# A streaming encoder step on one core: the scan's factors prepared in two parts beside the products, its widest level in two strips, and one gate block earlier in the order

## The chip, the core and the metric

The kernel runs on one core of one Trainium2 chip. The metric is device time in microseconds (us), the median of the runs shown. One program computes the whole step in one launch.

## The reference, cut to what matters

The step is one encoder layer for a prompt of 1024 rows and a sample of 64 rows, 1024 features wide. The combined projection `h @ w_in` feeds three groups of heads; the change is in the first, the gated scan of four heads with 128 features each:

```
def step(s, inp):                                  # one chunk of the sequence, one head
    qc, kc, vc, gc = inp
    G = cumsum(gc)                                 # running sum of log decay
    o = (qc * exp(G)) @ s                          # what the state gives
    att[t, u] = sum_k qc[t,k] * exp(G[t,k] - G[u,k]) * kc[u,k]    for u <= t
    o = o + att @ vc
    s_new = exp(G[-1]) * s + (kc * exp(G[-1] - G)).T @ vc
```

Afterwards each row of `o` is normalised and multiplied with a gate `silu(ag)`. The second group of heads has a gate `bg`, the third a gate `cg`, both also blocks of the combined projection.

## The kernel before, in words

**Order of the work.** Tasks are Python generators. A planner (`Sched`) keeps a planned clock for each engine, adds a written cost for every instruction, and always continues the first task whose inputs are ready on those clocks. The main task issues the projections: for each block of 128 weight columns (`names`, line 676) three chunks of columns (384, 384 and 320) with 24 matmuls each, three products (high and low halves) per 128 features. These are the rows `mm<-hhi,whi`, `mm<-hlo,whi` and `mm<-hhi,wlo`. They go out in batches of six, and between batches a scan task may put its own work. After that a tile scheduler fixes the place of each instruction on its engine.

**The scan of one head** (`hgrn`, line 364) is spawned when `ai` of its head has been projected and starts when V of the head stands in rows (`v{h}`). It has three groups: group 0 and 1 are four chunks of 128 prompt rows, group 2 is the sample's 64 rows. For each group:

- `prep` makes the factors. `G` is the running sum (line 383), `M = lnk - G`. For each level b of 64, 32, 16, 8, 4 and 2 a tile `E` gets its first halves from M and its second halves from G (two adds on DVE), goes through Exp on ACT, and its second halves are multiplied with q on DVE. Then come `k`, `qf` (with a copy of q on POOL, line 404), `Kh`, `eL` and `Qh` (which takes the place of G).
- `pe1` multiplies on PE. "pB" means one chunk's block of 32x32 products: 16 products `hg<-E` of the levels 16 to 2 and four `hg<-qf,k`; each counts twice in the trace (32 and 8). "pA" means the products of the levels 64 and 32 for all chunks: per chunk one 64x64 product and two 32x32 products. Four pB come first, with a planned pause of 0.9 us behind each, then pA, then four transposes of `Kh`. DVE turns pB into `AT` by a mask (`msk`), a sum (line 449) and a spread; ACT copies pA into `AT` and the transposed `Kh` into `Kt`.
- `pe2a` makes the states S by `V,Kt` and a chain on DVE; `pe2b` makes the output by `V,AT` and `S,G` and starts its norm: four squares on ACT (`o_sb`), two steps on POOL (`small`, lines 318 and 321), a product on DVE (`o_sb`); `pe3` transposes `o_sb` and applies the gate.

pA, pB, the states and the output all take banks of one PSUM tag, `hg`, with three buffers. `E` has seven buffers, `G` two, `M`, `k`, `qf` and `Kh` one.

**What a head's work follows.** The order is prep(0), pe1(0), prep(1), pe2a(0), pe2b(0), pe1(1), prep(2), pe2a(1), pe3(0), pe2b(1), pe1(2), pe3(1), pe2a(2), pe2b(2), pe3(2). The main task stops at `af` of head j until the scan of head j-2 has ended, and at `cg` j until that of head 1+j has ended. The gate blocks `cg` 0 and 1 and `bg` 0 and 1 stand behind the four heads' blocks.

Of the kernel before, what the change touches and what calls it, by code (L numbers as in the profile page):

```python
# [104 lines left out]
def hybrid_step(  # L105
# [47 lines left out]
    def ps_hg():  # L153
        return ps.tile([P, 512], F32, tag="hg", name="hg", bufs=3)
# [22 lines left out]
    def act(out, in_, func, **kw):  # L177
        t = TABLE.get(func)
        sw = 1.3 if t is not None and t != cur.get("table") else 0.0
        if t is not None:  # L180
            cur["table"] = t
        sch.op("ACT", 0.2 + sw + free(in_) / 1200.0)
        cur['ACT'] = ACT.activation(out, in_, func, **kw)  # L183

    def tt(out, a, b, op):
        sch.op("DVE", 0.07 + free(out) / 960.0)
        cur['DVE'] = DVE.tensor_tensor(out=out, in0=a, in1=b, op=op)  # L187

    def stt(out, a, s, b, op0, op1):
        sch.op("DVE", 0.07 + free(out) / 960.0)  # L190
        DVE.scalar_tensor_tensor(out=out, in0=a, scalar=s, in1=b, op0=op0, op1=op1)
# [9 lines left out]
    def sub(out, a, b):  # L201
        tt(out, a, b, ALU.subtract)
# [110 lines left out]
    def rstd_of(ms, n, w=1, more=None):  # L313

        r = small()
        sch.op("POOL", 0.6)
# [4 lines left out]
        POOL.tensor_tensor(out=r[:n, :w], in0=r[:n, :w], in1=mhalf[:n, :w], op=ALU.pow)  # L321
        return r
# [39 lines left out]


    def hgrn(h, st, hp, hgc):
        yield f"v{h}"
# [3 lines left out]
        S0 = hp([P, P], F32, "S0", 1)  # L369
        SP.dma_start(S0, state_hgrn[0, 0, h])  # L370
        ctxs = {}

        def prep(gi):
            t0, width, csz, v0 = groups[gi]
            nch = width // csz
            lf, lk, qq = logf[:, t0:t0 + width], lnk[:, t0:t0 + width], q[:, t0:t0 + width]

            def g(tag, bufs=1):
                return hp([P, 512], F32, tag, bufs)[:, :width]

            G = g("G", 2)
            sch.op("DVE", 0.07 + width / 480.0)
            DVE.tensor_tensor_scan(G, reset[:, :width], lf, 0.0, ALU.mult, ALU.add)
            M = g("M")
            sub(M, lk, G)
            Gc = G.rearrange("p (c t) -> p c t", t=csz)
            E = {}
            for b in LEVELS:
                if 2 * b > csz:
                    continue  # L390
                nb = width // (2 * b)
                e = g("E", 7)
                ev, gv, mv, qv = [x.rearrange("p (n two b) -> p n two b", two=2, b=b) for x in (e, G, M, qq)]
                ref = gv[:, :, 0, b - 1:b].broadcast_to([P, nb, b])
                tt(ev[:, :, 0, :], mv[:, :, 0, :], ref, ALU.add)
                tt(ev[:, :, 1, :], gv[:, :, 1, :], ref, ALU.subtract)
                act(e, e, AF.Exp)
                stt(ev[:, :, 1, :], ev[:, :, 1, :], QSCALE, qv[:, :, 1, :], ALU.mult, ALU.mult)
                E[b] = e
            k = g("k")  # L400
            act(k, lk, AF.Exp)
            qf = hp([P, 2, 512], F32, "qf")[:, :, :width]
            sch.op("POOL", 0.1 + width / 1000.0)
            POOL.tensor_copy(qf[:, 1, :], qq)  # L404
            act(qf[:, 0, :], lf, AF.Exp)
            stt(qf[:, 0, :], qf[:, 0, :], QSCALE, qq, ALU.mult, ALU.mult)
            Kh = g("Kh")
            tt(Kh.rearrange("p (c t) -> p c t", t=csz), M.rearrange("p (c t) -> p c t", t=csz),
               Gc[:, :, csz - 1:csz].broadcast_to([P, nch, csz]), ALU.add)
            act(Kh, Kh, AF.Exp)  # L410
            eL = hp([P, 4], F32, "eL", 2)
            act(eL[:, :nch], Gc[:, :, csz - 1], AF.Exp)
            Qh = G
            act(Qh, G, AF.Exp)
            stt(Qh, Qh, QSCALE, qq, ALU.mult, ALU.mult)
            ctxs[gi] = dict(E=E, k=k, qf=qf, Kh=Kh, eL=eL, Qh=Qh, qq=qq)

        def pause(us):

            sch.cur.dep["EV"] = sch.t["PE"] + us  # L420
            yield None

        def pe1(gi):

            t0, width, csz, v0 = groups[gi]
            nch, nq = width // csz, csz // 32
            x = ctxs[gi]
            E, k, qf, qq = x["E"], x["k"], x["qf"], x["qq"]
            AT = hp([P, 4, P], F32, "AT", 1)
            for c0 in range(0, nch, 2):  # L430
                cn = min(2, nch - c0)
# [17 lines left out]
                DVE.tensor_reduce(out=dg[:csz, :cn], in_=msk[:csz, :cn].rearrange("p c l t -> p c t l"), axis=AX.X,  # L449
                                  op=ALU.add)  # L450
# [3 lines left out]
            pA = ps_hg().rearrange("p (c t) -> p c t", t=P)  # L454
            for c in range(nch):
                o = c * csz
                if csz == P:
                    mm(pA[0:64, c, 64:128], E[64][:, o:o + 64], E[64][:, o + 64:o + 128], True, True)
                for s in range(0, csz, 64):
                    mm(pA[s:s + 32, c, s + 32:s + 64], E[32][:, o + s:o + s + 32], E[32][:, o + s + 32:o + s + 64],  # L460
                       True, True)
# [62 lines left out]
        prep(0)  # L524
        yield None
        yield from pe1(0)
        prep(1)
        yield None
        pe2a(0, None)
        yield None  # L530
        pe2b(0)
        yield from pe1(1)
        prep(2)
        yield None
        pe2a(1, ctxs[0]["S"][-1])
# [134 lines left out]
    def main():  # L670
# [724 lines left out]
```

## Time and profile before

| What | Value |
|---|---|
| median of 3 runs (lowest, highest) | 945.51 us (944.09, 945.72) |
| the profiled execution | 946.23 us |
| its span, first to last instruction | 944.5 us |
| mean granted TensorE clock | 0.996 of full speed |
| PE busy over the span | 98% |
| the scan's products on PE | about 158 to 436 us |

The profiled execution's time is 1.7 us more than its span. PE busy is an overlap of pipelined matmuls: in a stream of 384 columns a matmul is shown as 0.34 us long while the next one begins 0.17 us later. What a piece of work costs PE is therefore read from the starts of the rows around it, not from its busy time. PEclk is the share of full clock that PE was granted. "Idle before" in brackets behind a row says how long the engine had nothing in flight, and who released it.

### The profile page before, as it was taken

How to read it: one execution, taken by the hardware profiler on the slowest of the kernel's cores; microseconds unless marked ns; L12 is line 12 of the kernel's file. 1: busy time of each engine (PE TensorE's matmuls, PEld its weight loads, DVE VectorE, ACT ScalarE, POOL GpSimd, SP SyncE). 2: the span in 40 equal slices, each digit the busy share in tenths (PEclk: the TensorE clock that was granted, in tenths of full speed). 3: DMA queues.
4: the chain of work that ended last, by engine and by line, in shares of the span. 5: the costliest groups of instructions: out<-in, count | busy, mean ns of one | idle time of the engine just before them, and what ended most of it. 6: DMA issues, size and time to landing. Idle time of an engine off the chain costs nothing.

```text
span 944.5 us, 18234 instructions
## 1 busy us (share of the span) xinstructions
PE 923.9 (98%) x7440; PEld 863.0 (91%) x7440; DVE 554.9 (59%) x1125; ACT 474.7 (50%) x1002; POOL 106.7 (11%) x194
## 2 busy tenths in 40 slices
PE   8999999999999999999999999999999999999997
PEld 6899999999988998998879778999999999999997
DVE  7849472548648636663485678555574455573343
ACT  7623382957435746992574766343453333342231
POOL 5503330001001001000000000212110000001110
PEclk9999999999989999999999999999999999999999
DMA  8806410101010111011110420222542011232221
GB/s 306 270 20 198 144 45 25 46 24 54 24 46 9 46 38 41 24 46 62 57 37 32 145 74 25 89 90 90 168 123 88 25 45 46 68 112 90 90 94 64
DMA packets 33126, 73.60 MB, mean 78 GB/s; under 512 B 5601, under 2 KB 18065, under 8 KB 33042
## 3 DMA queue, kind: packets, MB, share of 16 engines
q1 hardware_dynamic: 30112, 68.07, 22.5%
q0 software_dynamic: 1888, 4.35, 1.3%
q8 instruction: 58, 0.95, 0.4%
q14 instruction: 26, 0.21, 0.1%
q10 hardware_dynamic: 1042, 0.01, 0.1%
HBM read 56.45 MB, written 15.89 MB: 77 GB/s over the span
## 4 chain that ended last, share of the span: by engine, by line
PE 83%; DVE 6%; DMA 4%; ACT 2%; issue 2%; POOL 2%; DVEq 0%; POOLq 0%; ACTq 0%
PE mm L171 64%; PE hg L171 15%; PE tp L175 5%; DVE sm L587 3%; DVE sm L187 1%; DVE wlo L187 1%; POOL small L321 1%; DMA wraw<-in_w_xk_dram 1%; DMA xt<-in_x_prompt_dram 1%; DMA mkd<-mraw 1%; DMA gT<-in_norm_mem_dram 1%; DMA wraw<-in_w_xv_dram 1%; DMA mvd<-mtm 0%; ACT whi L183 0%; DVE hlo L187 0%
## 5 line engine op out<-in xcount | busy, mean ns | idle before, releaser
L171 PE MATMUL mm<-hhi,whi 128*128 128x384 f32 (+2 forms) x1272 | 421.8, 332 | 0.0
L171 PE MATMUL mm<-hlo,whi 128*128 128x384 f32 (+2 forms) x1272 | 413.2, 325 | 0.0
L171 PE MATMUL mm<-hhi,wlo 128*128 128x384 f32 (+2 forms) x1248 | 406.0, 325 | 0.0
L171 PEld LDWEIGHTS mm<-hhi,whi 128*128 128x128 f32 x1272 | 239.5, 188 | 4.5 <-issue 1.1
L171 PEld LDWEIGHTS mm<-hlo,whi 128*128 128x128 f32 x1272 | 239.6, 188 | 1.2 <-issue 1.1
L171 PEld LDWEIGHTS mm<-hhi,wlo 128*128 128x128 f32 x1248 | 234.7, 188 | 0.5 <-issue 0.3
L183 ACT ACTIVATE whi<-wraw 128x1024 fp32r<-128x1024 f32 (+1 forms) x53 | 55.1, 1041 | 82.5 <-PE mm L171 66.9
L187 DVE TENSOR_TENSOR wlo<-wraw,whi 128x1024 fp32r<-128x1024 f32 (+1 forms) x53 | 63.6, 1202 | 44.3 <-ACT whi L183 44.0
L183 ACT ACT_TABLE_LOAD x63 | 80.8, 1283 | 6.1 <-issue 2.0
L183 ACT ACTIVATE wraw<-mm 128x384 f32<-128x384 f32 (+3 forms) x51 | 22.9, 450 | 72.7 <-PE mm L171 62.7
L587 DVE TENSOR_TENSOR_SCAN sm<-sm 128x384 f32<-128x384 f32 (+4 forms) x52 | 48.2, 936 | 14.3 <-ACT sm L183 14.3
L183 ACT ACTIVATE sm<-hg 128x384 f32<-128x384 f32 (+4 forms) x104 | 42.3, 485 | 16.2 <-PE hg L171 9.1
L187 DVE TENSOR_TENSOR wraw<-mm,gain 128x384 f32<-128x384 f32 (+1 forms) x48 | 24.4, 509 | 41.7 <-ACT wraw L183 41.5
L1176 POOL TENSOR_TENSOR small<-small 128x1 f32<-128x1 f32 (+1 forms) x18 | 4.2, 234 | 373.9 <-ACT wraw L183 373.9
L171 PE MATMUL mm<-mhi,wlo 128*128 128x256 f32 x128 | 36.0, 289 | 2.6 <-DVE wlo L187 2.5
L171 PEld LDWEIGHTS hg<-E 128*32 128x32 f32 (+1 forms) x1288 | 24.9, 113 | 14.2 <-issue 6.4
L321 POOL TENSOR_TENSOR small<-small,mhalf 128x1 f32<-128x1 f32 (+2 forms) x50 | 36.6, 733 | 4.2
L171 PE MATMUL mm<-mhi,whi 128*128 128x256 f32 x128 | 36.1, 289 | 0.6 <-ACT mhi L183 0.6
L171 PE MATMUL hg<-E 128*32 128x32 f32 (+1 forms) x1288 | 33.7, 203 | 1.7 <-DVE o_sb L187 1.7
L171 PE MATMUL mm<-mlo,whi 128*128 128x256 f32 x128 | 35.0, 282 | 0.0
L404 POOL COPY qf<-q 128x512 f32<-128x512 f32 (+1 forms) x12 | 14.1, 1179 | 181.9 <-PE hg L171 168.2
L187 DVE TENSOR_TENSOR wlo<-C,whi 128x1024 fp32r<-128x1024 f32 x16 | 19.6, 1225 | 25.1 <-ACT whi L183 23.6
(209 smaller groups left out, 1426.3 us busy)
## 6 DMA issues: line engine op xcount, KB each, us to landing
wraw<-in_w_in_dram SPq DMA_DIRECT2D x28, 512.0 KB, 3.6
xt<-in_x_prompt_dram SPq DMA_DIRECT2D x8, 512.0 KB, 6.5
wraw<-in_w_xv_dram SPq DMA_DIRECT2D x8, 512.0 KB, 4.1
wraw<-in_w_out_dram SPq DMA_DIRECT2D x8, 512.0 KB, 3.6
C<-in_x_prompt_dram SPq DMA_DIRECT2D x8, 512.0 KB, 3.6
x1d<-C SPq DMA_DIRECT2D x8, 512.0 KB, 2.9
wraw<-in_w_xq_dram SPq DMA_DIRECT2D x8, 512.0 KB, 3.6
wraw<-in_w_xo_dram SPq DMA_DIRECT2D x8, 512.0 KB, 3.5
```

What stands on the lines that cost most here:

```text
L171: cur['PE'] = PE.matmul(out, lhsT=lhsT, rhs=rhs, start=start, stop=stop, skip_group_check=True)
L175: PE.transpose(out, in_, ident[:n, :n])
L183: cur['ACT'] = ACT.activation(out, in_, func, **kw)
L187: cur['DVE'] = DVE.tensor_tensor(out=out, in0=a, in1=b, op=op)
L321: POOL.tensor_tensor(out=r[:n, :w], in0=r[:n, :w], in1=mhalf[:n, :w], op=ALU.pow)
L404: POOL.tensor_copy(qf[:, 1, :], qq)
L587: DVE.tensor_tensor_scan(m[:nq, :n][:, ::-1], m[:nq, :n][:, ::-1], m[:nq, :n][:, ::-1], 1.0 if p is None else p[:nq, 0:1], ALU.mult, ALU.min)
L1176: POOL.tensor_tensor(out=ms[:n, 0:1], in0=ms[:n, 0:1], in1=ms[:n, pi:pi + 1], op=ALU.add)
```

## The change

1. `prep` is cut in two. `prepA` makes G, M and the three widest levels, `prepB` the three narrow levels, `Kh`, `k`, `qf`, `eL` and `Qh`. Within a part all adds are issued first, then the Exp, then the products. `beside` gives a part its own planned readiness, so that the head's products don't wait for it in the plan.
2. `pe1` is cut in two. `pe1a` (pA) comes first and needs only the two widest levels; a pause; then `pe1b` (the four pB, the transposes).
3. The 64x64 product of pA becomes two products with 32 of its columns each (two strips of 32 output partitions).
4. The order is now pe1a(0), prepA(1), pe1b(0), pe2a(0), pe2b(0), prepB(1), pe1a(1), prepA(2), pe1b(1), pe2a(1), pe3(0), pe2b(1), prepB(2), pe1a(2), pe1b(2), and so on. prepA(0) of the next head may begin once pe1a(2) of this head is out, prepB(0) once pe2a(2) is; both before `v{h}`.
5. `bg` 0 moves from behind `cg` to behind head 1's blocks. Its three chunks of 24 matmuls follow `ag` 1.
6. The planned cost of the norm's POOL step grows with the number of columns; the copy of q on POOL loses its planned cost.

The products and their operands are the same apart from point 3; the number of ACT table loads goes from 63 to 66. From the first transposes of `kr` behind the scan on, PE's order is the same row for row.

```diff
+        def levels(gi, bs):
...
+            for b in bs:
+                e = buf(gi, "E", 7)
...
+                tt(ev[:, :, 0, :], mv[:, :, 0, :], ref, ALU.add)
+                tt(ev[:, :, 1, :], gv[:, :, 1, :], ref, ALU.subtract)
+                vs.append((e, ev, qv, sch.t["DVE"]))
...
+            for e, ev, qv, at in vs:
+                sch.fresh(DVE=at)
+                act(e, e, AF.Exp)
...
+                stt(ev[:, :, 1, :], ev[:, :, 1, :], QSCALE, qv[:, :, 1, :], ALU.mult, ALU.mult)
+        def prepA(gi):
...
+            DVE.tensor_tensor_scan(G, reset[:, :width], lf, 0.0, ALU.mult, ALU.add)
+            M = buf(gi, "M")
+            sub(M, lk, G)
...
+            levels(gi, split_levels(gi)[0])
+        def pe1a(gi):
...
+                    for i in range(0, 64, 32):
+                        mm(pA[i:i + 32, c, 64:128], E[64][:, o + i:o + i + 32], E[64][:, o + 64:o + 128], True, True,
+                           0.045)
...
-                    mm(pA[0:64, c, 64:128], E[64][:, o:o + 64], E[64][:, o + 64:o + 128], True, True)
...
+        if h:
+            yield ("wide", h - 1)
+        beside(prepA, 0)
+        if h:
+            yield ("narrow", h - 1)
+        beside(prepB, 0)
+        yield f"v{h}"
...
+        pe1a(0)
+        beside(prepA, 1)
+        yield from pause(0.9)
+        yield from pe1b(0)
...
         names += [("af", h), ("aq", h), ("ai", h), ("ag", h)]
-        names += [("cg", 0), ("cg", 1), ("bg", 0), ("bg", 1)]
+            if h == 1:
+                names += [("bg", 0)]
+        names += [("cg", 0), ("cg", 1), ("bg", 1)]
```

**PE, head 1, group 1, before:** the last two of four pB (`hg<-E 32x32 x16` with `hg<-qf,k`) and the start of pA (`hg<-E 64x64`).

```order
L171 MATMUL hg<-E 32x32 x16
L171 MATMUL hg<-qf,k 32x64 x4
L171 MATMUL hg<-E 32x32 x16
L171 MATMUL hg<-qf,k 32x64 x4
L171 MATMUL hg<-E 64x64
L171 MATMUL hg<-E 32x32 x2
L171 MATMUL hg<-E 64x64
```

The same place now: pA (`hg<-E 32x64 x2` are the two strips) between projection matmuls.

```order
L171 MATMUL mm<-hhi_107,wlo 128x384
L171 MATMUL hg<-E 32x64 x2
L171 MATMUL hg<-E 32x32 x2
L171 MATMUL hg<-E 32x64 x2
L171 MATMUL hg<-E 32x32 x2
L171 MATMUL hg<-E 32x64 x2
L171 MATMUL hg<-E 32x32 x2
L171 MATMUL hg<-E 32x64 x2
L171 MATMUL hg<-E 32x32 x2
L171 MATMUL mm<-hhi_109,whi 128x320
```

Before, the four pB and pA stood in one run right behind the output products of group 0; now pA stands alone, each pB has at least six projection matmuls on either side, and the transposes stand apart.

**DVE, head 2, group 0, before:** what stands ahead of the first `msk` of the group (`M<-fl,G` and `E<-M,G` belong to group 1; `wlo`, `L` and `fl` to the main task).

```order
L187 TENSOR_TENSOR M<-fl,G 128x512
L191 SCALAR_TENSOR_TENSOR G<-G,q 128x512
L187 TENSOR_TENSOR E<-M,G 128x4x64
L187 TENSOR_TENSOR wlo<-wraw,whi 128x1024
L199 COPY fl<-mm 128x320
L187 TENSOR_TENSOR E<-G 128x4x64
L191 SCALAR_TENSOR_TENSOR L<-fl,L 128x1088
L191 SCALAR_TENSOR_TENSOR E<-E,q 128x4x64
L187 TENSOR_TENSOR fl<-L,fl 128x1088
L187 TENSOR_TENSOR msk<-hg,fmask 128x384
```

The same place now (L416 is the running sum):

```order
L416 SCALAR_TENSOR_TENSOR G<-reset,L 128x512
L187 TENSOR_TENSOR M<-fl,G 128x512
L187 TENSOR_TENSOR E<-G 128x4x64
L187 TENSOR_TENSOR E<-M,G 128x4x64
L187 TENSOR_TENSOR E<-M,G 128x8x32
L187 TENSOR_TENSOR E<-G 128x8x32
L187 TENSOR_TENSOR E<-M,G 128x16x16
L187 TENSOR_TENSOR E<-G 128x16x16
L191 SCALAR_TENSOR_TENSOR E<-E,q 128x4x64
L191 SCALAR_TENSOR_TENSOR E<-E,q 128x8x32
L187 TENSOR_TENSOR msk<-hg,fmask 128x384
```

Six adds of group 1 and two of its products now stand ahead of group 0's `msk`, in the place of one level of group 1 and work of the main task.

**POOL, head 1, before:** the copies of q for group 2 and for the next head's group 0, ahead of the norm of group 1 (`small 128x4`).

```order
L404 COPY qf<-q 128x64
L404 COPY qf<-q 128x512
L318 TENSOR_SCALAR small<-small 128x4
L321 TENSOR_TENSOR small<-small,mhalf 128x4
L318 TENSOR_SCALAR small<-small 64x1
```

The same place now:

```order
L443 COPY qf<-q 128x64
L318 TENSOR_SCALAR small<-small 128x4
L321 TENSOR_TENSOR small<-small,mhalf 128x4
L443 COPY qf<-q 128x512
L318 TENSOR_SCALAR small<-small 64x1
```

The long copy for the next group went behind the norm of group 1 and stands ahead of that of group 2.

More of the change, by code (lines that the diff above doesn't have):

```diff
@@ L315, in rstd_of @@
         r = small()
-        sch.op("POOL", 0.6)
+        sch.op("POOL", 0.3 + 0.25 * w)
         if more is None:
@@ L364, in hgrn @@
     def hgrn(h, st, hp, hgc):
-        yield f"v{h}"
         logf, lnk, q, V = st["logf"], st["lnk"], st["q"], st["V"]
@@ L368, in hgrn, with beside, factors_of @@
         groups = [(0, 512, P, 0), (512, 512, P, 4), (SEQ, SMP, SMP, 8)]
-        S0 = hp([P, P], F32, "S0", 1)
-        SP.dma_start(S0, state_hgrn[0, 0, h])
         ctxs = {}
-        def prep(gi):
+        def beside(f, gi):
+            save = sch.cur.dep
+            sch.fresh(**ctxs.setdefault(gi, dict(dep={}))["dep"])
+            f(gi)
+            ctxs[gi]["dep"], sch.cur.dep = sch.cur.dep, save
+        def factors_of(gi):
+            for e, v in ctxs[gi]["dep"].items():
+                sch.cur.dep[e] = max(v, sch.cur.dep.get(e, 0.0))
@@ new lines, in buf @@
+        def buf(gi, tag, bufs=1):
+            return hp([P, 512], F32, tag, bufs)[:, :groups[gi][1]]
+        def levels(gi, bs):
+            x = ctxs[gi]
+            width = groups[gi][1]
+            vs = []
+            for b in bs:
+                e = buf(gi, "E", 7)
+                ev, gv, mv, qv = [y.rearrange("p (n two b) -> p n two b", two=2, b=b)
+                                  for y in (e, x["G"], x["M"], x["qq"])]
+                ref = gv[:, :, 0, b - 1:b].broadcast_to([P, width // (2 * b), b])
+                tt(ev[:, :, 0, :], mv[:, :, 0, :], ref, ALU.add)
+                tt(ev[:, :, 1, :], gv[:, :, 1, :], ref, ALU.subtract)
+                vs.append((e, ev, qv, sch.t["DVE"]))
+                x["E"][b] = e
+            ends = []
+            for e, ev, qv, at in vs:
+                sch.fresh(DVE=at)
+                act(e, e, AF.Exp)
+                ends.append(sch.t["ACT"])
+            for (e, ev, qv, _), at in zip(vs, ends):
+                sch.fresh(ACT=at)
+                stt(ev[:, :, 1, :], ev[:, :, 1, :], QSCALE, qv[:, :, 1, :], ALU.mult, ALU.mult)
@@ new lines, in split_levels @@
+        def split_levels(gi):
+            bs = [b for b in LEVELS if 2 * b <= groups[gi][2]]
+            return bs[:3], bs[3:]
+        def prepA(gi):
+            t0, width, csz, v0 = groups[gi]
+            lf, lk, qq = logf[:, t0:t0 + width], lnk[:, t0:t0 + width], q[:, t0:t0 + width]
+            G = buf(gi, "G", 2)
+            sch.op("DVE", 0.07 + width / 480.0)
+            DVE.tensor_tensor_scan(G, reset[:, :width], lf, 0.0, ALU.mult, ALU.add)
+            M = buf(gi, "M")
+            sub(M, lk, G)
+            ctxs[gi].update(G=G, M=M, qq=qq, lf=lf, lk=lk, E={})
+            levels(gi, split_levels(gi)[0])
@@ L374, in prep, with prepB @@
+        def prepB(gi):
             t0, width, csz, v0 = groups[gi]
             nch = width // csz
[L376 to L385, printed above, removed]
@@ L386, in prep @@
-            Gc = G.rearrange("p (c t) -> p c t", t=csz)
[L387 to L407, printed above, removed]
+            x = ctxs[gi]
+            G, M, qq, lf, lk = x["G"], x["M"], x["qq"], x["lf"], x["lk"]
+            Gc = G.rearrange("p (c t) -> p c t", t=csz)
@@ L408, in prep @@
+            Kh = buf(gi, "Kh")
             tt(Kh.rearrange("p (c t) -> p c t", t=csz), M.rearrange("p (c t) -> p c t", t=csz),
                Gc[:, :, csz - 1:csz].broadcast_to([P, nch, csz]), ALU.add)
+            qf = hp([P, 2, 512], F32, "qf")[:, :, :width]
+            levels(gi, split_levels(gi)[1])
+            sch.fresh()
+            k = buf(gi, "k")
+            act(k, lk, AF.Exp)
+            act(qf[:, 0, :], lf, AF.Exp)
             act(Kh, Kh, AF.Exp)
@@ L414, in prep @@
             act(Qh, G, AF.Exp)
+            stt(qf[:, 0, :], qf[:, 0, :], QSCALE, qq, ALU.mult, ALU.mult)
+            POOL.tensor_copy(qf[:, 1, :], qq)
             stt(Qh, Qh, QSCALE, qq, ALU.mult, ALU.mult)
-            ctxs[gi] = dict(E=E, k=k, qf=qf, Kh=Kh, eL=eL, Qh=Qh, qq=qq)
+            x.update(k=k, qf=qf, Kh=Kh, eL=eL, Qh=Qh)
         def pause(us):
@@ L421, in pause, with pe1b @@
             yield None
-        def pe1(gi):
+        def pe1a(gi):
+            t0, width, csz, v0 = groups[gi]
+            E = ctxs[gi]["E"]
+            pA = ps_hg().rearrange("p (c t) -> p c t", t=P)
+            for c in range(width // csz):
+                o = c * csz
+                if csz == P:
+                    for i in range(0, 64, 32):
+                        mm(pA[i:i + 32, c, 64:128], E[64][:, o + i:o + i + 32], E[64][:, o + 64:o + 128], True, True,
+                           0.045)
+                for s in range(0, csz, 64):
+                    mm(pA[s:s + 32, c, s + 32:s + 64], E[32][:, o + s:o + s + 32], E[32][:, o + s + 32:o + s + 64],
+                       True, True)
+            ctxs[gi]["pA"] = pA
+        def pe1b(gi):
             t0, width, csz, v0 = groups[gi]
@@ L427, in pe1 @@
             x = ctxs[gi]
-            E, k, qf, qq = x["E"], x["k"], x["qf"], x["qq"]
+            E, k, qf, pA = x["E"], x["k"], x["qf"], x["pA"]
             AT = hp([P, 4, P], F32, "AT", 1)
@@ L522, in pe3 @@
             stt(cs, pT[:, :nch, :csz], onorm[:, h:h + 1], cs, ALU.mult, ALU.mult)
-        prep(0)
+        if h:
[5 more added lines that the diff above has]
+        yield f"v{h}"
+        S0 = hp([P, P], F32, "S0", 1)
+        SP.dma_start(S0, state_hgrn[0, 0, h])
+        factors_of(0)
         yield None
-        yield from pe1(0)
-        prep(1)
+        pe1a(0)
+        beside(prepA, 1)
+        yield from pause(0.9)
+        yield from pe1b(0)
         yield None
@@ L531, in hgrn @@
         pe2b(0)
-        yield from pe1(1)
-        prep(2)
+        save = dict(ctxs[1]["dep"])
+        beside(prepB, 1)
+        for e, v in save.items():
+            sch.cur.dep[e] = max(v, sch.cur.dep.get(e, 0.0))
+        yield None
+        pe1a(1)
+        beside(prepA, 2)
+        factors_of(1)
+        yield from pause(0.9)
+        yield from pe1b(1)
         yield None
@@ L539, in hgrn @@
         pe2b(1)
+        beside(prepB, 2)
         SP.dma_start(p_hgrn[0, 0, h], ctxs[1]["S"][-1])
-        yield from pe1(2)
+        factors_of(2)
+        yield None
+        pe1a(2)
+        sch.done[("wide", h)] = 0.0
+        yield from pause(0.9)
+        yield from pe1b(2)
         yield None
@@ L544, in hgrn @@
         pe2a(2, S0)
+        sch.done[("narrow", h)] = 0.0
         yield None
```

7 lines of the change are left out of this document (removed).

## The prediction

> **What bounds the kernel now.** I read the page first, then the windows of the scan, then the timeline of PE piece by piece, the chain of waits through the one bad place, and the groups by shape.
>
> ```profile
> span 944.5 us, 18234 instructions
> PE 923.9 (98%) x7440; PEld 863.0 (91%) x7440; DVE 554.9 (59%) x1125; ACT 474.7 (50%) x1002; POOL 106.7 (11%) x194
> ```
>
> PE is the bound. A gain can come from three things only: PE waiting, PE running at a lower clock, PE needing less time for the same products. The windows (span, then busy time and count of PE, PEld, DVE, ACT, POOL, then PEclk) give the scan and one stretch in it:
>
> ```profile
> 158.00:436.00 278.00, 274.33 (x3006) 251.53 (x3005) 169.35 (x404) 180.37 (x354) 20.41 (x35) 0.99 0.11 35
> 278.00:284.80 6.80, 6.80 (x41) 6.25 (x40) 4.22 (x18) 2.56 (x11) 0.00 (x0) 0.50 0.01 2
> ```
>
> Over the scan's 278 us DVE and ACT are busy for 61% and 65%, so both have room on average. In the second row PE had half its clock for 6.8 us: 3.4 us lost. What stands around it, in the timeline of PE:
>
> ```profile
> 273.76 0.46 PE L171 MATMUL hg<-E 128*32 128x32 f32 x32
> ...
> 275.25 0.30 PE L171 MATMUL hg<-qf,k 128*32 128x64 f32 x6
> 277.23 2.76 PE L171 MATMUL hg<-E 128*64 128x64 f32 x24 [1.67 <-DVE o_sb L187]
> ...
> 291.74 0.66 PE L175 MATMUL tp<-ident,o_sb 128*128 128x128 f32 x4 [0.66 <-DVE o_sb L187]
> ```
>
> From 273.76 to about 275.35 the four pB of head 1, group 1, run in one piece: 0.39 us each. Then PE idles 1.67 us. The chain that ended last, from there:
>
> ```profile
> 275.41 1.05 POOL small L321
> 276.46 0.02 issue
> 276.48 0.70 DVE o_sb L187
> ...
> 287.89 1.32 POOL qf L404
> ...
> 289.92 1.05 POOL small L321
> ```
>
> pA's products wait there for `o_sb`: output, two pB and pA need four `hg` banks of three, and the output's bank comes free only behind POOL (1.05) and DVE (0.70). The second wait (0.66) has a copy of `qf` (1.32 us) ahead of the norm in POOL's queue. All waits of PE's loads for `o_sb` in the scan (total, times, longest):
>
> ```profile
> PEld tp L175 <- DVE o_sb L187: 3.9, 7, 1.0
> PEld hg L171 <- DVE o_sb L187: 2.1, 2, 1.8
> ```
>
> So 6.0 us in all, of which 1.8 and 1.0 are the two places above; 3.2 us are spread over the rest.
>
> What pieces cost at full clock, read between the starts of the matmuls around them (a 384-column matmul takes 0.17 us in a stream):
>
> ```profile
> 165.44 0.33 PE L171 MATMUL mm<-hhi,wlo 128*128 128x384 f32 x1
> 165.70 0.46 PE L171 MATMUL hg<-E 128*32 128x32 f32 x32
> 165.98 0.34 PE L171 MATMUL hg<-qf,k 128*32 128x64 f32 x8
> 166.25 0.44 PE L171 MATMUL mm<-hhi,whi 128*128 128x384 f32 x1
> 166.53 0.34 PE L171 MATMUL mm<-hlo,whi 128*128 128x384 f32 x1
> ...
> 167.22 0.34 PE L171 MATMUL mm<-hhi,wlo 128*128 128x384 f32 x1
> 167.49 1.84 PE L171 MATMUL hg<-E 128*64 128x64 f32 x24
> 169.27 0.66 PE L175 MATMUL tp<-ident,Kh 128*128 128x128 f32 x4
> 169.68 0.42 PE L171 MATMUL mm<-hhi,whi 128*128 128x384 f32 x1
> 169.94 0.34 PE L171 MATMUL mm<-hlo,whi 128*128 128x384 f32 x1
> ```
>
> A pB standing alone: 166.53 - 165.44 - 2 x 0.17 = 0.75 us. In a run it took 0.39, so going into and out of these narrow products costs PE about 0.35 us. pA with the transposes: 169.94 - 167.22 - 0.35 = 2.37 us, 1.78 of it (167.49 to 169.27) for 24 instructions, where a pB starts 32 in 0.28 us (165.70 to 165.98). That is the 64-wide product between 32-wide ones. [...]
>
> **The change part by part.** All terms are against the profiled execution, 946.2 us (0.7 over the median).
>
> *1. The break in head 1.* With pA ahead of the pB it takes the third bank, and 48 projection matmuls (24 of 384 columns, 24 of 320) stand between pA and the next pB; the run without projections is gone, and `bg` 0 gives the main task work there while it waits for head 0. The two waits and the half clock go: 1.67 + 0.66 + 3.4 = -5.7. Next late would be the second pB's bank, covered by those 48 matmuls (24 x 0.17 = 4.1 us for the wider half alone, against 1.05 + 0.70 and the squares).
>
> *2. The other waits for `o_sb`.* For the two large groups the transposes of `o_sb` now stand behind pA, pB, or more than 30 matmuls, and the norm of group 1 is ahead of the long `qf` copy on POOL. For the 64 rows only 6 to 12 matmuls (1.0 to 2.1 us) cover the chain in heads 1 to 3, so about 1.0 us stays: 3.2 - 1.0 = -2.2. If the cover fails everywhere, 0.
>
> *3. The strips.* pA becomes 32 instructions, all 32 wide. In a pB, each of the four column strips gets eight `E` in 0.28 us (0.035 each) and two `qf` in the remaining 0.11 (0.055 each; 64 columns like the new strips). The busiest strip of pA gets two of each per chunk: 0.18 x 4 + 0.35 = 1.07 us alone. The transposes now stand apart; the same kind alone:
>
> ```profile
> 219.10 0.44 PE L171 MATMUL mm<-hhi,whi 128*128 128x384 f32 x1
> 219.38 0.66 PE L175 MATMUL tp<-ident,o_sb 128*128 128x128 f32 x4
> 219.80 0.42 PE L171 MATMUL mm<-hlo,whi 128*128 128x384 f32 x1
> 220.06 0.34 PE L171 MATMUL mm<-hhi,wlo 128*128 128x384 f32 x1
> ```
>
> 220.06 - 219.10 - 0.35 = 0.61. So 2.37 becomes 1.07 + 0.61, eight times: -5.5. Bounds for pA: as fast as a pB's 32 `E` (0.28 + 0.35 = 0.63), or strips that don't overlap at all (4 x 0.36 + 0.35 = 1.79): -9.0 to +0.2. I take 1.07, since pB shows both kinds overlapping across strips.
>
> *4. More pieces.* Each narrow piece that newly stands alone costs the 0.35 us. The four pB of group 1 in heads 1 and 3 stood in runs (in head 3 with little between): 8 x 0.35 = 2.8. Group 2's two products of pA, its pB and its transpose stand alone in three heads (in head 3 they remain one run): 9 x 0.35 = 3.2 at most, nothing at least, for the old runs already changed width between them; I take half. Together +4.4 (2.8 to 6.0).
>
> *5. New waits on DVE.* The wide levels of the next group now stand ahead of `msk`. Rows by shape:
>
> ```profile
> L383 DVE TENSOR_TENSOR_SCAN G<-reset,L 128x512 f32<-128x512 f32 x8 | 9.6, 1215 | 0.9 <-PE hg L171 0.9
> L187 DVE TENSOR_TENSOR M<-fl,G 128x512 f32<-128x512 f32 x8 | 5.6, 698 | 0.1
> L187 DVE TENSOR_TENSOR E<-G 128x256 f32<-128x256 f32 x48 | 20.4, 424 | 0.0
> L191 DVE SCALAR_TENSOR_TENSOR E<-E,q 128x256 f32<-128x256 f32 x48 | 19.2, 419 | 15.7 <-ACT E L183 15.3
> L449 DVE TENSOR_REDUCE dg<-msk 128x64 f32<-128x384 f32 x16 | 13.3, 830 | 0.1
> L183 ACT ACT_TABLE_LOAD x63 | 80.8, 1283 | 6.1 <-issue 2.0 <-DVE small L1211 1.8 <-PE hg L171 1.0
> ```
>
> 1.22 + 0.70 + 6 x 0.42 + 2 x 0.42 = 5.3 us stand before `msk`; `msk` (between an add's 0.42 and M's 0.70), sum (0.83) and spread (0.42) of two pB then take about 1.8. PE needs `AT` for `V,AT` at the end of the group, behind pA, four pB (4 x 0.75), six times six matmuls (36 x 0.17 = 6.3) and the transposes (0.6): 9.9 us, `V,Kt` not counted. DVE fits in most groups; before, one level with `wlo`, `L` and `fl` stood at the same place. I take +2.0 in all; between 0 and what the second rival gives.
>
> *6. The rest at nothing.* Three more table loads are 3 x 1.28 = 3.8 us of ACT's 98 idle us in the scan; without that cover they would lie on the path once each. `bg` 0's matmuls are only moved; at the end `bq`'s 72 matmuls fill head 3's tail as before. SP's loads of S0 and stores of S stand between weight loads as before, and each weight block has a block's 12 us of lead. Behind the scan PE's order is unchanged, so a gain there is kept; matmuls around 36 us that change places at the start can bring 0.5 us either way.
>
> Sum: -5.7 - 2.2 - 5.5 + 4.4 + 2.0 = -7.0. The profiled execution would take 939.2 us, the median of the runs 938.5 us.
>
> **The rivals.**
>
> *No gain from the strips.* If strips wait for each other, term 3 is +0.2 and the sum -1.3: 944.2. For it: all strips use all 128 rows. Against it: pB's 32-wide products do the same and start every 0.009 us. I give it 0.06.
>
> *DVE becomes the bound, slower.* In the plan a 256-column add costs 0.34 us, in the trace 0.42, so the plan sends PE on too early when DVE has a burst. Per large group DVE has, between pA and `V,AT`: 5.3, twice 1.8, the six narrow adds (2.5) and `Kh` (0.7 like M): 12.1 us against PE's 9.9, so 2.2 us per group where DVE has no lead; eight groups, 18 us. It decides from 9/8 = 1.1 us per group (the sum without term 5 is -9.0). At 2.2 per group the time is 945.5 - 9.0 + 18 = 954.5. For it: the same queue order in all eight groups. Against it: DVE is busy 61%, and what it does early isn't owed later. Chance 0.11.
>
> *Half clock again somewhere.* The row of 0.50 followed an idle time of only 1.67 us among narrow products. One such place, about 2 us of wait and 3.4 of clock, makes the sum -1.6: 943.9. [...] Against it: every narrow piece now has projections on both sides, and rows like those at 165 us kept the full clock. Chance 0.04.
>
> **How the numbers follow.** The forecast, -7.0 with its bounds, has 0.75; another 0.04 goes to strips at their lower bound with hardly any new wait (about -11.7: 933.8 and under). Faster, slower or no change I count from 0.2% (1.9 us), about what a measurement of this kernel can tell. Faster: 0.75 + 0.04 = 0.79. Same: 0.06 + 0.04 = 0.10. Slower: 0.11. The range goes from 933 (terms 3 and 5 near their good ends) to 944.5 (takes in the first and third rival and leaves out the second).
>
> **What would show it.** Right: no stretch at 0.50 in the scan; no wait of 1 us or more for `o_sb` on PE; pA standing alone at 0.9 to 1.3 us; the scan's end some 7 us earlier and everything behind it shifted unchanged. Wrong: pA near 1.8 us (first rival); PE waits for `AT`, `S` or `E` of about 1 us in each large group (second); a PEclk of 0.50 (third). If the time is gained before 158 us or behind 436 us, the argument is wrong whatever the total.

## The result, and the profile after

The changed kernel takes 935.1 us (median of 4 runs, 933.8 to 937.42) where the kernel before takes 945.62 on the same chip: a ratio of 0.9884, 95% interval 0.9862 to 0.9907. It is 10.5 us faster. The forecast was 938.5 (933.0 to 944.5).

The first lines of the page, and the windows of the scan (span, then busy time and count of PE, PEld, DVE, ACT, POOL, then PEclk, the DMA share and GB/s):

```profile
span 933.3 us, 18372 instructions
PE 914.2 (98%) x7504; PEld 853.6 (91%) x7504; DVE 556.6 (60%) x1125; ACT 479.5 (51%) x1005; POOL 107.2 (11%) x194
```

```profile
150.00:424.00 274.00, 272.44 (x3119) 249.51 (x3118) 172.51 (x406) 186.71 (x361) 20.80 (x35) 1.00 0.12 38
```

PE is still the bound, and busy for 9.7 us less. The granted clock of the scan is 1.00: the stretch at 0.50 is gone. To see where the time came from, I cut the span at two marks of PE's order that no edit moves: the first transpose of V (`tp<-ident,vT`), with which head 0 begins, and the first `tp<-ident,kr`, with which the heads behind the scan begin. Of the kernel before:

```profile
137.40:451.30 313.90, 310.23 (x3222) 287.16 (x3221) 175.49 (x413) 189.82 (x373) 20.41 (x35) 0.99 0.13 39
451.30:944.50 493.20, 482.25 (x3326) 452.21 (x3323) 281.07 (x538) 212.31 (x521) 35.98 (x72) 1.00 0.24 79
```

Of the changed kernel:

```profile
138.70:440.10 301.40, 299.84 (x3285) 276.67 (x3284) 177.34 (x413) 194.27 (x376) 20.80 (x35) 1.00 0.13 40
440.10:933.30 493.20, 482.17 (x3325) 452.08 (x3323) 281.04 (x538) 212.35 (x521) 35.96 (x72) 1.00 0.24 79
```

The scan went from 313.9 to 301.4 us, 12.5 less; what lies behind it took 493.20 us in both. The 1.2 us that are lost ahead of the scan are less than the start moves by itself: profiled again, the same changed kernel reached the first mark at 141.9, 3.2 us later, and its run was 3.3 us longer. The stretch between the marks was 301.5 there. So the scan's stretch repeats within a few tenths while the start moves by 3 to 4 us; below it is the finer measure, and the medians of whole runs are given beside it.

One caution goes with the kernel before. Its 6.8 us at 0.50 alone bring the mean granted clock of 944.5 us down by 0.0036, and the profiled execution shows 0.996. Of the 33 executions of it beside the experiments, 21 had a mean of 0.997 or more, which leaves no room for such a stretch; their median is 945.3 us, that of the other 12 is 946.5. So the 3.4 us are no fixed part of its time. This is part of why gains against its profiled scan come out larger than gains of the medians: 12.5 against 10.5 us here, 7.9 against 6.1 and 4.7 against 2.8 in the first two experiments.

The waits of PE's loads in the scan of the changed kernel (total, times, longest):

```profile
PEld hg L171 <- issue: 12.8, 55, 0.3
PEld hg L171 <- ACT Kt L183: 2.2, 6, 0.6
PEld tp L175 <- DVE o_sb L187: 1.7, 3, 0.9
```

`o_sb` fell from 6.0 to 1.7, and no wait reaches 1 us. What is new is ACT's `Kt` (0.2 before). The row `issue` is time in which a load waited for nothing that the profile shows (7.5 us, 34 times before). A wait of the loads can pass while matmuls are still in flight; the time that PE itself is shown idle is less, and what a wait costs can lie between the two. Before, and now:

```profile
PE tp L175 <- DVE o_sb L187: 1.7, 5, 0.7
PE hg L171 <- DVE o_sb L187: 1.7, 1, 1.7
```

```profile
PE tp L175 <- DVE o_sb L187: 0.8, 2, 0.6
PE hg L171 <- ACT Kt L183: 0.6, 2, 0.3
```

That is 3.4 us before and 1.4 now. What the pieces cost, in the timeline of PE around head 1, group 0:

```profile
224.81 0.34 PE L171 MATMUL mm<-hhi,wlo 128*128 128x384 f32 x1
225.08 0.89 PE L171 MATMUL hg<-E 128*32 128x64 f32 x32
225.90 0.44 PE L171 MATMUL mm<-hhi,whi 128*128 128x384 f32 x1
226.18 0.33 PE L171 MATMUL mm<-hlo,whi 128*128 128x384 f32 x1
...
235.44 0.34 PE L171 MATMUL mm<-hhi,wlo 128*128 128x384 f32 x1
235.61 0.60 PE L175 MATMUL tp<-ident,Kh 128*128 128x128 f32 x4
235.97 0.42 PE L171 MATMUL mm<-hhi,whi 128*128 128x384 f32 x1
236.23 0.34 PE L171 MATMUL mm<-hlo,whi 128*128 128x384 f32 x1
```

pA alone: 226.18 - 224.81 - 0.35 = 1.02 us (1.07 forecast). The transposes alone: 236.23 - 235.44 - 0.35 = 0.44 us (0.61 forecast).

### The profile page after: what moved, and what is told of

Read it like the earlier page. It is cut to its first block, busy times and chain, and to the rows that moved or that the text cites. A ratio compares the mean times of both kernels' runs of the same rounds, so it can differ in the third digit from the quotient of the medians.

```text
span 933.3 us, 18372 instructions
## 1 busy us (share of the span) xinstructions
PE 914.2 (98%) x7504; PEld 853.6 (91%) x7504; DVE 556.6 (60%) x1125; ACT 479.5 (51%) x1005; POOL 107.2 (11%) x194
## 4 chain that ended last, share of the span: by engine, by line
PE 82%; DVE 6%; ACT 4%; DMA 4%; issue 2%; POOL 1%; DVEq 0%; POOLq 0%; ACTq 0%
PE mm L171 64%; PE hg L171 14%; PE tp L175 5%; DVE sm L650 3%; DVE sm L187 1%; DVE wlo L187 1%; ACT L183 1%; ACT whi L183 1%; DMA xt<-in_x_prompt_dram 1%; DVE hlo L187 1%; DMA wraw<-in_w_xk_dram 1%; DMA mkd<-mraw 1%; DMA wraw<-in_w_xo_dram 1%; DMA gT<-in_norm_mem_dram 1%; DMA mvd<-mtm 1%
## 5 line engine op out<-in xcount | busy, mean ns | idle before, releaser
L183 ACT ACTIVATE E<-E 128x512 f32<-128x512 f32 (+1 forms) x68 | 32.8, 515 | 10.5 <-DVE E L187 9.9
L191 DVE SCALAR_TENSOR_TENSOR C<-wraw,small,C 128x384 f32<-128x384 f32 (+3 forms) x54 | 27.8, 569 | 10.2 <-POOL small L321 10.2
```

## The experiments

All kernels by the two marks: time to the first mark, the scan's stretch, the rest (profiled run), then the median and its ratio to the kernel before on the same chip.

| kernel | start | scan | rest | median | ratio (95%) |
|---|---|---|---|---|---|
| before | 137.5 | 313.9 | 493.2 | 945.62 | |
| changed | 138.7 | 301.4 | 493.2 | 935.1 | 0.9884 (0.9862-0.9907) |
| changed, again | 141.9 | 301.5 | 493.1 | 935.23 | 0.9883 (0.9862-0.9903) |
| changed, one 64x64 | 138.9 | 309.2 | 493.1 | 942.83 | 0.9966 (0.9950-0.9982) |
| before + strips | 138.2 | 306.0 | 493.5 | 939.56 | 0.9937 (0.9917-0.9958) |
| gate block back | 140.6 | 299.5 | 493.9 | 935.47 | 0.9884 (0.9865-0.9903) |
| pA last | 138.3 | 304.1 | 493.1 | 936.66 | 0.9900 (0.9876-0.9925) |
| no early begin | 138.1 | 304.4 | 493.2 | 937.3 | 0.9913 (0.9890-0.9935) |
| pairs | 136.4 | 301.9 | 493.0 | 935.2 | 0.9884 (0.9866-0.9902) |
| Kt first | 139.8 | 303.1 | 493.1 | 937.08 | 0.9906 (0.9883-0.9930) |
| pairs, Kt first | 137.1 | 297.9 | 493.1 | 930.9 | 0.9841 (0.9818-0.9863) |
| the same, again | 141.0 | 297.6 | 493.2 | 931.17 | 0.9841 (0.9824-0.9858) |
| four in a row, Kt first | 136.3 | 301.2 | 493.2 | 933.19 | 0.9862 (0.9843-0.9880) |
| pairs, Kt first, gate back | 140.8 | 298.2 | 493.2 | 930.92 | 0.9851 (0.9824-0.9878) |

### The strips by themselves: taken out of the changed kernel, put into the one before

Out of the changed kernel, with the planned cost kept so that PE's order stays:

```diff
-                    for i in range(0, 64, 32):
-                        mm(pA[i:i + 32, c, 64:128], E[64][:, o + i:o + i + 32], E[64][:, o + 64:o + 128], True, True,
-                           0.045)
+                    mm(pA[0:64, c, 64:128], E[64][:, o:o + 64], E[64][:, o + 64:o + 128], True, True, 0.09)
```

> The changed kernel with the widest level again as one 64x64 product per chunk (its planned cost kept, so that every other instruction keeps its place). Theory of the strips: going from 64-wide to 32-wide products and back costs PE in each chunk, so pA alone takes about 1.95 us instead of 1.01, eight times: +7.4 us, about 942.5, with no new waits. Rival, that the order did it (pA first, filled waits): pA stays within 0.15 us of 1.01, the time within 1 us of 935.1.

It took 942.83, with a scan of 309.2: 7.8 us more than with strips. The timeline shows pA at the same place:

```profile
227.02 0.34 PE L171 MATMUL mm<-hhi,wlo 128*128 128x384 f32 x1
227.28 1.84 PE L171 MATMUL hg<-E 128*64 128x64 f32 x24
229.06 0.45 PE L171 MATMUL mm<-hhi,whi 128*128 128x384 f32 x1
229.34 0.34 PE L171 MATMUL mm<-hlo,whi 128*128 128x384 f32 x1
```

229.34 - 227.02 - 0.35 = 1.97 us against 1.02, and 8 x 0.95 = 7.6. The theory holds, and the rival of strips that wait for each other falls.

Into the kernel before, nothing else changed:

```diff
-                    mm(pA[0:64, c, 64:128], E[64][:, o:o + 64], E[64][:, o + 64:o + 128], True, True)
+                    for i in range(0, 64, 32):
+                        mm(pA[i:i + 32, c, 64:128], E[64][:, o + i:o + i + 32], E[64][:, o + 64:o + 128], True, True,
+                           0.0625)
```

> The kernel before with the strips alone (order, parts and gate blocks as before). Theory of the strips: pA with its transposes goes from 2.37 to about 1.45 us, eight times: -7.4 us, about 938; the stretch at 0.50 clock in head 1 and its wait for o_sb stay. Rival, that the order did it: 945 or more; a second rival, that strips only pay where PE's next work is ready, gives -2 to -4.

It took 939.56, scan 306.0, 7.9 us less than before. Against expectation the half clock went as well. Its waits, and the place of the old break (pA of head 1's group 1, behind its four pB):

```profile
PEld tp L175 <- DVE o_sb L187: 4.9, 8, 1.3
PEld hg L171 <- ACT AT L183: 2.3, 3, 1.2
PEld hg L171 <- DVE o_sb L187: 1.7, 2, 1.4
PEld hg L171 <- ACT Kt L183: 1.2, 4, 0.4
```

```profile
275.38 0.89 PE L171 MATMUL hg<-E 128*32 128x64 f32 x32 [1.28 <-DVE o_sb L187]
```

The break is there, but PE idles 1.28 us in it instead of 1.67, and the clock stays whole (1.00 from 275 to 290). The kernel before had, beside its 6.0 us for `o_sb`:

```profile
PEld hg L171 <- ACT AT L183: 0.6, 2, 0.4
...
PEld hg L171 <- ACT Kt L183: 0.2, 1, 0.2
```

PE's pieces became shorter, and the waits for `o_sb`, `AT` and `Kt` rose from 6.0 + 0.6 + 0.2 to 6.6 + 2.3 + 1.2 us. So 3.3 us of what the strips gave went to waits. pA with its transposes takes 1.41 us in this kernel's timeline: 8 x (2.37 - 1.41) = 7.7 less, 3.4 less of half clock, and 3.3 more of waits (the 0.4 saved in the break are in them) make -7.8, and -7.9 was measured. So strips alone give 7.9 and the order alone (the kernel with one 64x64) 4.7, which is about the 12.5 of both. That the sum fits is partly chance: each alone removes the half clock, which can go only once, and the order returns the 3.3 us that strips alone lose.

### The gate block put back

```diff
-            if h == 1:
-                names += [("bg", 0)]
-        names += [("cg", 0), ("cg", 1), ("bg", 1)]
+        names += [("cg", 0), ("cg", 1), ("bg", 0), ("bg", 1)]
```

> The changed kernel with the gate block bg 0 back behind cg. Theory that pA ahead of pB removes the bank wait by itself: no wait of 1 us or more for o_sb on PE, no 0.50 in the scan, within 1.5 us of 935.1. Rival, that the moved block's 72 matmuls are what fills head 1: a wait of 1.5 us and the half clock return there, +3 to +5.7 us, 938 to 941.

935.47: no difference in the medians, no half clock in the scan, `o_sb` 0.5 us. The block isn't needed to remove the break. By the scan's stretch (299.5) the changed kernel would even be 1.9 us shorter without the move, of which 0.7 were lost again behind the scan (493.9). `Kt` waits 1.1 us instead of 2.2, and the profile shows no idle time of PE itself in the scan, against 1.4 us in the changed kernel. So the gain looks like one of single waits; the last experiment tests this.

### pA behind the pB, and no early begin

Two other parts of the new order undone, each alone. pA behind the four pB of its group:

```diff
+            pe1a(gi)
+            pA = x["pA"]
             if csz == P:
                 act(AT[0:64, :nch, 64:128], pA[0:64, :nch, 64:128], AF.Copy)
...
-        pe1a(0)
...
-        pe1a(1)
...
-        pe1a(2)
```

> The changed kernel with pA behind the four pB of its group, where it stood in the kernel before; factors, strips and gate blocks as changed, nothing is left out. Theory (pA ahead of the pB is what removed the waits for the bank): the waits of PE's loads for o_sb go from 1.7 us back to 4 to 6 us and AT is later by pA's copies (ACT, two per group), so the time rises by 3 to 5 us: 938 to 940, and by 3.4 us more if the clock is halved once. Rival (the factors' order and the early begin did it, and pA's place is free): o_sb stays under 2.5 us and the time at 935 +- 0.7.

936.66, scan 304.1: 2.7 us more than changed, and a median between the two statements. In kind that was the theory (pA's place matters), but not by its mechanism. The waits:

```profile
PEld hg L171 <- ACT Kt L183: 3.0, 6, 1.1
PEld tp L175 <- DVE o_sb L187: 2.1, 4, 0.8
PEld hg L171 <- DVE S L191: 1.1, 2, 0.6
```

`o_sb` stays low (2.1 against 1.7), so the bank that pA takes early is not what removed these waits: with pA last, `Kt` and `S` come late instead. That pA's and the transposes' copies then reach ACT together at the group's end would explain it; this is argued from the order and not shown.

A head's first factors prepared only when V stands:

```diff
-        if h:
-            yield ("wide", h - 1)
+        yield f"v{h}"
         beside(prepA, 0)
-        if h:
-            yield ("narrow", h - 1)
         beside(prepB, 0)
-        yield f"v{h}"
```

> The changed kernel without the early begin: a head's first factors are prepared only when its projections are there, as in the kernel before; all else as changed, nothing is left out. Theory (PE has projections of the next head to run while DVE and ACT prepare, so the early begin hides work that is hidden anyway for heads 0 to 2, and pays only where the projections run short, in head 3): the time rises by 0 to 3 us, to 935 to 938, and the added idle time of PE stands in head 3. Rival (DVE and ACT set when a head begins; each head's begin is late by the 5.3 us of its wide factors less what projections cover): PE waits for E of 1 us or more at the begin of several heads, 940 or more.

937.3, scan 304.4: 3.0 us, within the theory, but the time isn't idle time in head 3 alone. `Kt` waits 5.6 us in place of 2.2, in heads 1, 2 and 3:

```profile
PEld hg L171 <- ACT Kt L183: 5.6, 8, 1.4
PEld tp L175 <- DVE o_sb L187: 2.9, 5, 0.9
```

PE does not wait for `E`, as the rival had it, but for the copy `Kt`. Where it waits longest (1.4 us, head 2), ACT runs the Exp of `k` and `qf` from 316.61 to 317.66 and the copy right behind them; in head 1 the copy stands behind those into `AT`. That the later factors put this work ahead of the copy is argued from ACT's order and not shown.

### Pieces: pairs, and Kt ahead

The pause behind each pB moved behind each pair:

```diff
-                    yield from pause(0.9)
+                yield from pause(0.9)
```

> The changed kernel without the pause between the two pB of a pair, so that they stand in one piece. Theory that each narrow piece costs PE 0.35 us for going in and out: 16 pieces fewer, -5.6 us, about 929.5. Rival, that the pauses cover waits for banks and for DVE: what is saved comes back as waits of PE for E, AT or banks, 934 to 938, or as a stretch at 0.50.

935.2, scan 301.9. A pair costs 1.12 us in place of 2 x 0.745, so the 0.37 per piece is confirmed (16 pairs, 5.9 us), and nothing of it arrives:

```profile
PEld hg L171 <- ACT Kt L183: 5.8, 6, 1.3
PEld tp L175 <- DVE o_sb L187: 1.4, 3, 1.1
```

With two stretches of projections fewer between the pB and `V,Kt`, the copy is late: PE's own idle time for `Kt` is 4.0 us, against 0.6. In time and in kind the rival holds, though `Kt` was not among the waits that it named. If so, moving the transposes and the copy ahead of the pB should help twice: alone, and with pairs.

```diff
             AT = hp([P, 4, P], F32, "AT", 1)
+            pk = ps_tp()
+            for c in range(nch):
+                tr(pk[:csz, c * P:(c + 1) * P], x["Kh"][:, c * csz:(c + 1) * csz], P)
+            Kt = hp([P, 512], F32, "Kt")
+            act(Kt[:csz, :nch * P], pk[:csz, :nch * P], AF.Copy)
             for c0 in range(0, nch, 2):
...
-            pk = ps_tp()
-            for c in range(nch):
-                tr(pk[:csz, c * P:(c + 1) * P], x["Kh"][:, c * csz:(c + 1) * csz], P)
-            Kt = hp([P, 512], F32, "Kt")
-            act(Kt[:csz, :nch * P], pk[:csz, :nch * P], AF.Copy)
```

> The changed kernel with the transposes of Kh and the copy Kt moved ahead of the four pB; nothing is left out. In the changed kernel PE's loads wait 2.2 us for ACT's Kt in the scan (6 times, longest 0.6), since the copy's transposes stand only some 6 to 12 matmuls (1 to 2 us) ahead of V,Kt. Theory (the new waits of the change come from the distance between the transposes and V,Kt, not from DVE): with the pB between them the waits for Kt go to under 0.3 us, V,Kt costs 0.90 us everywhere, and the time falls by 1.5 to 2.5 us: 933 us where the changed kernel shows 935.1. Rival (Kt is late because ACT's queue is full; what ends the wait then is E or AT a little later): waits for Kt fall and waits for AT, E or Kh grow by as much; 935 +- 0.7.

Alone it was a miss: 937.08, scan 303.1, 1.7 us more. `Kt` is gone from the waits and `V,Kt` costs 0.9 us wherever it stands alone, as the theory says, but `o_sb` rose from 1.7 to 4.2 us:

```profile
PEld tp L175 <- DVE o_sb L187: 4.2, 5, 1.2
```

The waits stand ahead of the last group's transpose of `o_sb`: PE itself idled 0.43, 0.93 and 0.66 us there in heads 0, 1 and 2, and in head 3's tail, where projections have run out, one wait of 0.49 came to the one of 0.55 that stays. In head 1 ACT begins the squares for this `o_sb` only at 298.80, 4.2 us behind the output product that starts at 294.64, with work for the next head and the projections ahead of them. Neither statement had that. With pairs as well:

> The changed kernel with both edits: the four pB of a large group in two pairs, each pair in one piece of PE's order, and the transposes of Kh and the copy Kt ahead of them; nothing is left out. With pairs alone the pieces became 0.37 us per pair cheaper (16 pairs, 5.9 us) while the waits for Kt grew from 2.2 to 5.8 us, and the time stayed at 935.2. Theory (the saving of a pair is real and was eaten by Kt, whose transposes had lost two stretches of projections as cover): with Kt ahead the waits for Kt are under 0.5 us and the time is 5 to 7 us under that of the changed kernel, about 929. Rival (DVE's sums and spreads of two pB coming together are late for V,AT; the wait moves from Kt to AT): waits for AT of 0.3 us or more per large group, 2.5 to 4 us in all, and 932 to 935.

930.9, scan 297.9, 4.2 and 3.5 us under the changed kernel: the theory's mechanism, with less than the 5 to 7 us it gave. Against Kt first alone it is 5.2 us in the scan and 6.2 in the median, around the 5.9 of the pairs. The first pair with its transposes, head 0, group 1:

```profile
177.63 0.31 PE L171 MATMUL mm<-hhi,wlo 128*128 128x320 f32 x1
177.78 0.60 PE L175 MATMUL tp<-ident,Kh 128*128 128x128 f32 x4
178.31 0.46 PE L171 MATMUL hg<-E 128*32 128x32 f32 x32
...
179.24 0.41 PE L171 MATMUL mm<-hhi,whi 128*128 128x320 f32 x1
179.49 0.31 PE L171 MATMUL mm<-hlo,whi 128*128 128x320 f32 x1
```

179.49 - 177.63 - 2 x 0.145 (320 columns) = 1.57 us: 1.13 for the pair and 0.44 for the transposes, which cost beside the narrow piece what they cost alone. The largest waits left are `o_sb`, 3.2 us (5 times, longest 0.9), and `S`, 0.8; none for `AT` as the rival had it.

> Pairs and Kt first once more, beside the changed kernel on the same chip. If the 4.4 us between their ratios to the kernel before (0.9841 and 0.9884) are real, it is 930 to 932 here and the changed kernel 934 to 936, and the ratios' intervals lie apart; if they were chance, both show the same time within 1 us.

> The changed kernel once more on the chip of these runs, unchanged: 934 to 936 us by its first four runs.

931.17 and 935.23 side by side; the intervals lie apart (0.9824 to 0.9858, and 0.9862 to 0.9903). Pairs with Kt first is a version faster than both kernels, by 4 us to the changed one.

### Four in a row, and the half clock again

```diff
-                yield from pause(0.9)
+                if csz < 0:
+                    yield None
```

> The kernel with pairs and Kt first, and the pause between the pairs taken out as well: the four pB of a large group stand in one piece behind the transposes of Kh; nothing is left out. A pair costs 1.12 us and a pB 0.745, so four cost 1.12 + 2 x 0.38 = 1.9 us against 2.24 for two pairs: 8 x 0.35 = 2.8 us less, 928. Theory (the three hg banks set how many narrow products may follow each other: pA holds one, so the third pB waits for the first msk, and the fourth for the second, which stands behind a sum and a spread on DVE): waits of PE for msk of about 0.3 and 1.3 us per large group, more than 1 us each at the fourth pB, so 1.2 us more per group in all, about 940, and 3.4 us more for each time that the clock is halved. Rival (DVE keeps up, and the break of the kernel before came from its o_sb alone): 928.

933.19, scan 301.2: 3.3 to 3.6 us more than with pairs by the scan, 2.0 to 2.3 by the medians. The theory of banks fails in most groups. Its premise was off: the kernel takes one bank for two pB, so pA and four pB need just the three. Head 1, group 1:

```profile
232.00 0.34 PE L171 MATMUL mm<-hhi,wlo 128*128 128x384 f32 x1
232.17 0.60 PE L175 MATMUL tp<-ident,Kh 128*128 128x128 f32 x4
...
234.42 0.41 PE L171 MATMUL mm<-hhi,whi 128*128 128x320 f32 x1
234.67 0.31 PE L171 MATMUL mm<-hlo,whi 128*128 128x320 f32 x1
```

234.67 - 232.00 - 0.32 = 2.35 us, 0.44 + 1.91: four pB cost 1.91, as if no bank were missing. So it is in five of the eight groups; in three it took 0.85 to 1.4 us more, for which the profile names no releaser (in one of them PE idles behind the pB, ahead of a projection). All eight are 22.2 us against 8 x (1.57 + 1.13) = 21.6 at the price of pairs: no gain, and no large loss. The 3.4 us came at one place, in head 1 (PE, then windows):

```profile
266.59 0.27 PE L175 MATMUL tp<-ident,o_sb 64*128 64x64 f32 x1 [1.70 <-DVE o_sb L187]
```

```profile
263.58:267.00 3.42, 1.72 (x10) 1.34 (x9) 3.02 (x5) 2.41 (x7) 1.89 (x2) 1.00 0.14 38
267.00:270.41 3.41, 3.41 (x14) 3.41 (x14) 3.41 (x11) 2.79 (x4) 2.46 (x1) 0.50 0.00 0
```

PE idled 1.70 us ahead of the last group's `o_sb`, and then the clock was 0.50 for 3.41 us: 1.7 + 1.7 = 3.4 lost. That is what the old break looked like, at another place and without a narrow product beside it.

### Pairs and Kt first, with the gate block back

> Pairs and Kt first, with bg 0 back behind cg as in the kernel before; nothing is left out. The time from the first vT transpose to the first kr transpose repeats within 0.3 us between profiled runs of the same kernel (301.4 and 301.5, 297.9 and 297.6), while the time ahead of it moves by 3 to 4. By this stretch bg 0 back alone was 1.9 us shorter (299.5 against 301.4), which the medians of whole runs could not show. If that is the gate block itself (more projections left for where PE waits), the stretch is 295.5 to 296.5 here and the time 929 to 930; if it was the place of single waits (Kt 1.1 instead of 2.2 us, o_sb 0.5 instead of 1.7), the stretch is 297 to 299, since Kt no longer waits here, and the time 930 to 932.

The edits are those shown above. 930.92, scan 298.2: the second statement. Where `Kt` no longer waits, `bg` 0's place is worth nothing, which agrees with the 1.9 us of the gate block alone being the place of single waits.

## Why the prediction was right, and where its sizes were wrong

The direction held, and so did the strips' mechanism: no 0.50 in the scan, no wait for `o_sb` of 1 us, pA alone at 1.02 us (0.9 to 1.3 asked), and the rest behind the scan unchanged at 493.20. The scan gave 12.5 us where the sum had 7.0; 1.2 were hidden by the start. That the median lies as near as 3.4 us to the forecast is partly luck, for the scan alone missed it by 5.5. Term by term:

1. **The break in head 1, -5.7.** In the profiled executions it went as said. The reason given (pA takes the third bank, `bg` 0 gives work) is not borne out: with the gate block back, and with pA last, the break does not return, and strips alone already remove the 3.4 us of half clock. Undone one at a time, none of the parts tried brought it back (the cut of the factors was not undone), so what removed the wait for the bank stays open. At this break the clock was halved behind 1.67 us of idle time and kept behind 1.28 (strips alone), and by the mean clocks above the kernel before did not lose it in every execution.
2. **The other waits for `o_sb`, -2.2.** They fell from 3.2 to 1.7: -1.5.
3. **The strips, -5.5.** 8 x (2.37 - 1.02 - 0.44) = -7.3, and 7.6 to 7.8 by the experiment. pA was right to 0.05 us. The term was mis-sized by the transposes: the quoted row at 219.38 gave 0.61 us, and without what stood beside it they cost 0.44. DVE finished that `o_sb` only at 219.33, and the projection ahead, the first behind the 64-row products `S,G`, held PE for 0.28 us instead of 0.17. The old pA was dear beside a pB: 1.78 / 4 = 0.44 us per chunk, which has 6 rows in the trace, where a whole pB in a run took 0.39 for 40.
4. **More pieces, +4.4.** This step failed: next to nothing was paid. The price of a narrow piece was right (0.35 forecast, 0.37 by the pairs), but the runs of before were not free of it. The long run in head 1, read without the half clock in the kernel with strips alone, took 5.59 us without its break against 6.45 for its parts standing alone, 0.9 saved and not 1.4; that of head 3 saved about 0.3. Group 2's pieces, with what stood in one run with them, cost 4.63 us before and 4.34 apart in head 0, 3.37 and 2.99 in head 1, 4.23 and 4.34 in head 2. The runs alternated between narrow and 128-wide products; that they paid at the changes is an estimate from these times.
5. **New waits, +2.0.** The size was right by the waits of the loads, the engine wrong: ACT's `Kt` (+2.0) in place of DVE's queue. Read between the starts of the rows, `V,Kt` cost some 1.6 us more in all than eight times its 0.89. Of the second rival nothing is seen: no wait of PE's loads for `E` or `msk` stands among those of the changed kernel's scan.

Terms 1, 2, 3 and 5 make -5.7 - 1.5 - 7.3 + 2.0 = -12.5, all that was measured, and leave nothing for term 4. Counted by PE's own idle time in place of the waits of its loads, it is -3.4 of half clock, -2.0 of idle time (3.4 to 1.4) and -7.3, together -12.7, which leaves +0.2: none or a few tenths for term 4, by either count. The large misses are terms 3 and 4, 1.8 and 4.4 us, both too cautious. The third rival, half clock elsewhere, didn't occur in the changed kernel's scan, but did in the one with four pB in a row, where it cost 3.4 us (1.70 of idle time, 1.7 of clock).

## What to carry to other kernels

Price a piece by where it stands: here a narrow piece among wide products cost about 0.35 us more, but a run that alternates between narrow and wide paid about as much as its pieces did apart. When PE's pieces get cheaper, look at once at what has lost its cover (here the copy `Kt` and the norm of `o_sb`): strips alone gave 3.3 us back, pairs alone gave all of it back, and pairs with the copy moved ahead gave 4 us. Cut the span at marks that no edit moves before comparing: the part in question repeated within 0.3 us, where whole runs of one kernel differed by 3 to 6.

## What the runs showed of the hardware

**The stretches at 0.50 begin whole steps of 3.413 us apart.** The stretch in the scan of the kernel before lasts 6.82 us, the one near 8 us in the changed kernel 3.41 (8.13 to 11.55), the one in the scan with four in a row 3.41. In the kernel before they begin at 277.98 and 943.57, 195.0 times 3.413 us apart, in the changed kernel at 8.13 and 929.74, 270.0 times, and with four in a row at 7.58, 267.00 and 929.18, 76.0 and 194.0 times. The last of each runs to the end of the span. Counted back to the span's start in steps of 3.413, these begins come to 1.5, 1.3 and 0.8 us in the three traces; that this differs from run to run fits the kernel before not losing the 3.4 us in every execution. The kernel before, the 3.42 us ahead of its half clock and the 6.82 us at 0.50:

```profile
274.56:277.98 3.42, 1.68 (x103) 1.27 (x91) 2.12 (x9) 2.28 (x9) 1.46 (x3) 1.00 0.46 158
277.98:284.80 6.82, 6.82 (x42) 6.27 (x40) 4.24 (x18) 2.58 (x11) 0.00 (x0) 0.50 0.01 2
```

PE was busy for 1.68 of 3.42 us there, and 1.72 of 3.42 with four in a row. With strips alone the wait of 1.28 us at the same break left PE busy for 2.46 us from 274.43 to 277.84, and it cost only itself. But the busy share alone does not tell. Near 34 us, ahead of the scan, the kernel with the gate block back kept its clock with 1.62 of 3.42:

```profile
34.28:37.70 3.42, 1.62 (x14) 1.41 (x12) 1.45 (x2) 1.06 (x1) 0.72 (x2) 1.00 0.87 334
37.70:41.11 3.41, 3.09 (x27) 3.12 (x28) 3.41 (x5) 2.95 (x5) 2.08 (x4) 1.00 0.59 171
```

What separates this from the two places at half clock isn't settled.

**The late starts go with a longer row of PE.** A row of PE at about 6 us, `hg<-rows,ones` (four products), took 1.98 to 2.21 us in nine of the fourteen traces and 3.77 us in five, among them the changed kernel's second profile (1.98 and 3.77), though the profile gives PEclk as 1.00 there in all of them. These five reached the first mark at 139.8 to 141.9 us, the nine at 136.3 to 138.9. That PE ran at about half pace there in these five is an estimate from 3.77 / 1.98 = 1.9; the granted clock does not show it. The stretch at 0.50 near 8 us stands in six of the other nine. What decides between them is open.
